# The last expert of each group is moved to the end, and its tokens are finished in slot order

## The chip, the cores and the metric

The kernel runs on one core of one Trainium2 chip. The metric is the device time of one execution in microseconds (us), the median of several runs. Before the change three runs took 882.38, 878.52 and 880.90 us: a median of 880.9.

## The reference, cut to what matters

The kernel computes one layer of a hybrid backbone (an S5 state-space branch and a convolution branch, merged, with a gated residual add), then a mixture of experts, then a final RMSNorm. The change touches only what stands behind the router. 512 tokens of 1024 channels choose one group of four and then two experts among the eight of that group:

```python
gate = jnp.sum(jax.nn.one_hot(expert_id, N_EXPERTS) * weights[..., None], axis=1)
out = jnp.zeros_like(h)
for e in range(N_EXPERTS):                      # 32 = 4 groups of 8
    act = jax.nn.silu(h @ w_gate[e]) * (h @ w_up[e])
    out = out + gate[:, e:e + 1] * (act @ w_down[e])
...
x = x + gt2 * out
return rmsnorm(x, g_final)
```

Both experts of a token lie in the same group. So a token can have at most one of the experts 7, 15, 23 and 31, the last of each group, and its other expert is then another one.

## The kernel before, in words

**Routing.** Each expert has up to 128 slots for its tokens. Tables on the chip hold, for each expert and slot, the token's row (`ix`, for gathers) and the row of its result in `ybuf` (`ixh`, for scatters; `ybuf` in device memory has two rows for each token, one for each of its experts, and is addressed in halves of 512 channels). `pw` holds the two weights of each token, `rk` its slot, `ex` its experts, `size` a size class for each expert. x after the first sub-layer lies in device memory as `x1d`, the normed and modulated rows as `h2d`.

**The expert loop** (lines 1632 to 1673, e from 0 to 32). Iteration e works on two experts at once: the down projection of expert e-1 and the gate and up projection of expert e. The orders of PE, ACT and DVE are written out by hand (`manual_schedule`, line 1621), so these three run what the loop says in the order in which it says it:

- `gather_e` (line 1397): POOL gathers the token rows of an expert two ahead into one of two buffers (`xgs`) by an indirect DMA.
- `tile_act` (1352): ACT computes Silu of the gate half, DVE multiplies by the up half, for expert e-1.
- `tile_gu` (1347): PE multiplies the tokens of expert e by its gate and up weights. An expert works in two parts of 64 slots; the second is skipped when the expert has at most 64 tokens (`halves`, 1408).
- `tile_at` (1358): PE transposes the product of `tile_act`, ACT copies it out of PSUM.
- `tile_x` (1329): PE transposes the gathered rows of expert e+1, ACT and DVE each copy one half.
- `tile_down` (1367): PE multiplies by the down weights into `pd`.
- `tile_y` and `scatter_e` (1376, 1415): DVE multiplies `pd` by the layer's output gate, POOL scatters the rows into `ybuf` by an indirect DMA. No scatter waits for another expert's scatter.

SP and POOL are not in the hand-written order. A planner puts their instructions into queues by when it expects each to be ready; a queue then runs in that order, and an instruction that waits holds up what is behind it. A size test (`halves`) on POOL is a branch: one indirect DMA for the first 64 slots, and a second one only for an expert with more.

**Weights.** `load_p(m)` issues the loads of 1 MB each on SP, three for each expert, some six experts ahead. They land in a ring of 20 places (`eraw` and `part_load`, 989 to 1022), made of several small pools of buffers; a load waits until the matmuls that read its place before are done. What the end of the kernel needs (x, the rows of `ybuf`, `g_final`) comes from the same ring. The last weight load is issued at 789.3 us.

**The end.** The results of experts 30 and 31 aren't scattered. POOL builds a one-hot matrix of slots and tokens for each (`last_prepare`, 1529), PE transposes it (`last_turn`, 1536), DVE and ACT make two parts of the weighted result (`last_y`, 1549), and PE adds these to the tokens' rows in PSUM (`fin`): x by a matmul with the identity (`last_x`, 1575), the two experts' rows by the one-hot matrix (`last_own`, 1580), the rows from `ybuf` (`last_mix`, 1587: ACT scales one row of a token, DVE adds the other, PE adds the sum). `last_rows` (1564) loads both rows of all tokens from `ybuf`, 4 loads of 1 MB on SP, after every scatter has landed. Then, for each of four blocks of 128 tokens: ACT sums squares (`last_sum`, 1594), DVE and ACT make 1/rms (`last_root`, `last_norm`), DVE scales, and SP stores 512 KB.

## Time and profile before

| | |
|---|---|
| median of 3 runs | 880.9 us |
| the profiled execution | 880.24 us |
| its span in the trace | 878.5 us |
| PE busy | 738.2 us (84%) |
| DVE busy | 458.5 us (52%) |
| ACT busy | 321.2 us (37%) |
| POOL busy | 329.6 us (38%) |
| mean granted TensorE clock | 0.959 of full speed |

The span is what the profiler recorded on the core; the device time of the same execution is 1.74 us longer. PE is TensorE, DVE VectorE, ACT ScalarE, POOL GpSimd, SP SyncE. Busy time is an average over stages with different limits, so the rows further down are taken from the stage that the change touches, the expert loop (from about 546 us) and the end.

The loop's iterations take 8.46 us each when both experts have at most 64 tokens. The down projection of expert 27 ends at 814.25 us, that of expert 31 at 849.24 us, and the span ends 29.26 us later.

### The profile page before, as it was taken

To read this page: it belongs to the slowest core of one execution; us is meant where nothing else is said; L and a number is where in the kernel's file an instruction comes from. 1 tells how busy PE (TensorE), PEld (TensorE's weight loads), DVE (VectorE), ACT (ScalarE), POOL (GpSimd) and SP (SyncE) were. 2 spreads that over 40 slices of the span, in tenths; PEclk is the share of its full clock that TensorE was granted. 3 is DMA by queue.
4 is the path that set the end of the run, shared out by engine and by line. 5 is a ranking of instruction groups with operands and counts; after the bars stand their busy time and mean duration, and the time that the engine had idled before them with its cause. 6 is when DMAs were issued, how large, how long until landed. Compare 5 with 4: busy or idle time off the path is not lost. (4 is left out here: it accounts for less than half of the span.)

```text
span 878.5 us, 14308 instructions
## 1 busy us (share of the span) xinstructions
PE 738.2 (84%) x5486; PEld 513.4 (58%) x5486; DVE 458.5 (52%) x723; ACT 321.2 (37%) x559; POOL 329.6 (38%) x293
## 2 busy tenths in 40 slices
PE   3498986998978986979999993788998998888885
PEld 0376863665656775746778872455655655555542
DVE  3948565355397798725985576133223232332344
ACT  3442621355465748526632331221112112121133
POOL 4647435345486697621610122122122122221400
PEclk9998997999989999989999996899999999999999
DMA  8916870342145454478687437999989998998042
GB/s 308 272 47 194 196 230 22 106 126 73 48 140 174 150 177 130 137 241 322 202 297 274 156 121 314 394 392 398 381 304 388 406 360 332 387 397 295 18 192 95
DMA packets 84679, 202.01 MB, mean 230 GB/s; under 512 B 12860, under 2 KB 42622, under 8 KB 74867
## 3 DMA queue, kind: packets, MB, share of 16 engines
q1 hardware_dynamic: 76754, 180.00, 57.7%
q0 software_dynamic: 5856, 12.45, 4.0%
q10 hardware_dynamic: 1984, 8.44, 3.6%
q8 instruction: 53, 0.87, 0.4%
q14 instruction: 32, 0.25, 0.1%
HBM read 180.16 MB, written 26.69 MB: 235 GB/s over the span
## 5 line engine op out<-in xcount | busy, mean ns | idle before, releaser
L1350 PE MATMUL peg<-eraw,st 128*64 128x256 f32 x1152 | 132.8, 384 | 8.4 <-PEq L1411 6.8
L1350 PEld LDWEIGHTS peg<-eraw,st 128*64 128x64 f32 x1152 | 94.1, 138 | 58.8 <-issue 33.9
L1335 DVE COPY st<-pxt 128x512 f32<-128x512 f32 x32 | 22.1, 691 | 158.7 <-PE pxt L1333 158.7
L1364 ACT ACTIVATE at<-pat 128x256 f32<-128x256 f32 x32 | 12.3, 383 | 216.0 <-PE pat L1362 216.0
L1322 POOL DMA_INDIRECT xg<-h2d,tb x32 | 30.3, 948 | 141.3 <-PE pxt L1333 129.9
L396 PE MATMUL zp<-hh,zuwh 128*128 128x512 f32 x192 | 78.2, 407 | 0.0
L398 PE MATMUL zp<-hh,zuwl 128*128 128x512 f32 x192 | 76.2, 397 | 0.5 <-POOL zuwl L757 0.4
L397 PE MATMUL zp<-hl,zuwh 128*128 128x512 f32 x192 | 76.0, 396 | 0.0
L1370 PE MATMUL ped<-eraw,at 128*64 128x512 f32 x288 | 68.9, 603 | 0.0
L98 POOL TENSOR_TENSOR adacc<-adacc,wa 128x512 f32<-128x512 f32 x30 | 47.2, 1574 | 40.9 <-ACT wa L857 38.7
L1405 POOL DMA_INDIRECT ybuf<-ye,ixh x34 | 33.9, 996 | 69.2 <-DVE ye L1380 41.6
L1380 DVE TENSOR_TENSOR ye<-ped,gt2h 128x512 f32<-128x512 f32 x60 | 39.0, 686 | 39.7 <-PE ped L1370 38.5
L1333 PE MATMUL pxt<-ident,xg 128*128 128x128 f32 x256 | 42.3, 303 | 8.5 <-DMA xg<-h2d,tb 7.7
L396 PEld LDWEIGHTS zp<-hh,zuwh 128*128 128x128 f32 x192 | 36.9, 192 | 11.7 <-issue 4.4
L398 PEld LDWEIGHTS zp<-hh,zuwl 128*128 128x128 f32 x192 | 36.7, 191 | 9.8 <-POOL zuwl L757 1.8
L1333 PEld LDWEIGHTS pxt<-ident,xg 128*128 128x128 f32 x256 | 33.6, 194 | 13.5 <-issue 9.0
L397 PEld LDWEIGHTS zp<-hl,zuwh 128*128 128x128 f32 x192 | 36.8, 192 | 7.1
L1362 PE MATMUL pat<-ident,sge 64*128 64x64 f32 x128 | 21.3, 286 | 19.0 <-PEq L1411 18.3
L1362 PEld LDWEIGHTS pat<-ident,sge 64*128 64x128 f32 x128 | 17.7, 209 | 32.8 <-PEq L1411 30.5
L1370 PEld LDWEIGHTS ped<-eraw,at 128*64 128x64 f32 x288 | 17.8, 136 | 27.2 <-issue 23.6
L98 POOL TENSOR_TENSOR vb<-vta,vtb 128x512 f32<-128x512 f32 x16 | 21.9, 1366 | 31.3 <-PE pv L533 20.2
L757 DVE TENSOR_TENSOR zuwl<-zr,zuwh 128x1024 fp32r<-128x1024 f32 x16 | 28.4, 1778 | 4.6 <-ACT zuwh L756 4.5
(499 smaller groups left out, 1652.7 us busy)
## 6 DMA issues: line engine op xcount, KB each, us to landing
eraw<-in_w_exp_gate_dram SPq DMA_DIRECT2D x24, 1024.0 KB
...
```

Source lines behind the costliest of these rows:

```text
L98: G.tensor_tensor(o, a, b, op=op)
L396: T.matmul(acc, lhsT=wh, rhs=ah, start=start, stop=False)
L397: T.matmul(acc, lhsT=wh, rhs=al, start=False, stop=False)
L398: T.matmul(acc, lhsT=wl, rhs=ah, start=False, stop=stop)
L757: (G if t in ZPOOL else V).tensor_tensor(zu[t][1], raw, zu[t][0].bitcast(F32), op=ALU.subtract)
L1322: G.indirect_dma_start(out=xg, out_offset=None, in_=h2d, in_offset=bass.IndirectOffsetOnAxis(ap=idx, axis=0), bounds_check=L - 1, oob_is_e ...
L1333: T.transpose(pt[:, k, :], xg[:, 4 * h + k:D:8], ident)
L1350: T.matmul(pg[H[c], 256 * a:256 * a + 256], lhsT=st[:, k, H[a]], rhs=r[c][k // 4][:, 256 * (k % 4):256 * (k % 4) + 256], start=(k == 0), s ...
L1362: T.transpose(pa[:, 128 * k + 64 * a:128 * k + 64 * a + 64], sg[64:128, 256 * a + k:256 * a + 256:2], ident[64:128, 64:128])
L1370: T.matmul(pd[a][H[c]], lhsT=at[:, 128 * k + 64 * a:128 * k + 64 * a + 64], rhs=r[2][k][:, 512 * c:512 * c + 512], start=(k == 0), stop=(k ...
L1380: V.tensor_tensor(y[:, 512 * a:512 * a + 512], pd[a], gt2h, op=ALU.mult)
L1405: return G.indirect_dma_start(out=ybuf.rearrange("r (c n) -> (r c) n", c=2), out_offset=bass.IndirectOffsetOnAxis(ap=ixh[:, a, e:e + 1], a ...
```

## The change: what it does

**Order.** The experts are computed in a new order (`ORD`): first the 28 that aren't the last of their group, then 7, 15, 23 and 31 (`DIR`). Weights, gathers, sizes and scatters follow this order. In the inputs these four have 9, 92, 10 and 13 tokens (counted by running the reference's router); experts 8, 9, 14 and 15 are the ones with more than 64. So expert 15 moves from place 15 to place 29.

**Results of the last four.** They aren't scattered to `ybuf`, and the one-hot matrices and the matmuls of the end (`last_prepare`, `last_turn`, `last_y`, `last_own`, `last_x`) are gone. Instead, for each of the four experts, POOL gathers in slot order: the tokens' rows of x and their weights (`own_rows`), then, once all scatters have landed, the result of each token's other expert (`own_other`). Ten indirect DMAs are issued for the first (one expert of the four needs two halves) and five for the second. Before that, four tiles of 128x2048 are cleared (`own_alloc`). DVE adds weight times other result to x (`own_base`); when the expert's down projection is done, DVE adds its weighted result and ACT sums the squares (`own_sum`); 1/rms follows (`roots`, `recip`), DVE scales and POOL scatters the rows to the output (`own_out`).

**All other tokens** are finished in token order during the last experts: `last_scale` and `last_mix` (ACT, DVE, and an add on POOL) for blocks 0 and 1 in iteration 30 and for 2 and 3 in iteration 31, `last_sum` in iterations 31 and 32, `last_out` at the end. `last_out` is now an indirect DMA on POOL whose list of rows leaves out the tokens of the last four experts.

**Tables.** `last_tables` replaces `last_weights` in iteration 1: 20 small DVE operations in place of 6, and two DMAs on SP that write the weights by result row to device memory (`pwd`).

**Places.** The loads of x and `g_final` move to the end of iteration 26, `own_alloc` and `own_rows` stand at the end of iteration 27, `last_rows` and `own_other` at the end of 28.

The diff, cut to its core (the removed functions, which stand in the code above, are left out):

```diff
+    EPG = NE // NGR
+    DIR = tuple(range(EPG - 1, NE, EPG))
+    ND = len(DIR)
+    ORD = [x_ for x_ in range(NE) if x_ not in DIR] + list(DIR)
...
-            eraws.setdefault(e, []).append(part_load((w_exp_gate, w_exp_up, w_exp_down)[m % 3][0, e], *a))
+            eraws.setdefault(e, []).append(part_load((w_exp_gate, w_exp_up, w_exp_down)[m % 3][0, ORD[e]], *a))
...
+    tok = mz2.tile([128, NT], F32, name="tok")
+    G.iota(tok, pattern=[[128, NT]], base=0, channel_multiplier=1, allow_small_or_imprecise_dtypes=True)
...
-            more[e] = nc.values_load(size[0:1, e:e + 1], engines=[EN.Pool], min_val=0, max_val=len(SIZES) - 1, skip_runtime_bounds_check_because=BYC)
-            by_size(e, lambda n: gather(xgs[e % NXG][0:n], ix[0:n, 0, e:e + 1]))
+            x_ = ORD[e]
+            more[e] = nc.values_load(size[0:1, x_:x_ + 1], engines=[EN.Pool], min_val=0, max_val=len(SIZES) - 1, skip_runtime_bounds_check_because=BYC)
+            by_size(e, lambda n: gather(xgs[e % NXG][0:n], ix[0:n, 0, x_:x_ + 1]))
...
+    ssf = mz2.tile([128, 2, 12], F32, name="ssf")
+    GRP = ((0, 6), (6, 10), (10, 12))
+    BC = (0, 1, 6, 7)
+    DC = (2, 4, 8, 10)
...
+    def after_all(ld):
+        for p_ in scattered:
+            tc.add_manual_dep(ins_of(ld), ins_of(p_).name, mybir.DependencyInfo(mybir.DependencyClass.Sync, mybir.DependencyReason.DATA), reason="results of every expert")
...
+    pwd = dram.tile([4 * L, 2], F32, name="pwd")
+    def last_tables():
+        pwt = mz2.tile([128, 2, NE], F32, tag="ixs", name="pwt", bufs=1)[:, 0].rearrange("p (q i c w) -> p q i c w", q=2, i=NT, c=2)
+        sp = mz2.tile([128, 2, NE], F32, tag="ixe", name="sp", bufs=1)
+        for q in range(2):
+            for w in range(2):
+                V.tensor_copy(pwt[:, q, :, :, w], pw[:, :, (q + w) % 2:(q + w) % 2 + 1].to_broadcast([128, NT, 2]))
+            SY.dma_start(out=bass.AP(pwd.tensor, pwd.offset + 4 * L * q, [[4, 128], [512, NT], [1, 4]]), in_=pwt[:, q].rearrange("p i c w -> p i (c w)"))
+        f = sp[:, 0, 0:24].rearrange("p (k a j) -> p k a j", k=3, a=2)
+        own["ix"] = mz2.tile([128, 3, 2, ND], I32, name="lix")
+        V.tensor_copy(f[:, 0], ixh[:, :, EPG - 1:NE:EPG])
+        V.tensor_scalar(f[:, 1], f[:, 0], float(2 * L), float(2 * L), op0=ALU.is_ge, op1=ALU.mult)
+        V.tensor_tensor(f[:, 2], f[:, 0], f[:, 1], op=ALU.subtract)
+        V.tensor_copy(own["ix"][:, 1], f[:, 2])
+        V.tensor_tensor(f[:, 2], f[:, 2], f[:, 1], op=ALU.subtract)
+        V.tensor_scalar(f[:, 2], f[:, 2], float(2 * L), None, op0=ALU.add)
+        V.tensor_copy(own["ix"][:, 2], f[:, 2])
+        V.tensor_copy(own["ix"][:, 0], f[:, 0])
+        d = sp[:, 1, 0:16].rearrange("p (k i q) -> p k i q", k=2, i=NT)
+        V.tensor_scalar(d[:, 0], ex, float(DIR[0]), None, op0=ALU.is_equal)
+        for x_ in DIR[1:]:
+            V.scalar_tensor_tensor(d[:, 0], ex, float(x_), d[:, 0], op0=ALU.is_equal, op1=ALU.add)
+        V.scalar_tensor_tensor(d[:, 1], rk, 128.0, d[:, 0], op0=ALU.is_lt, op1=ALU.mult)
+        V.tensor_tensor(d[:, 0, :, 0], d[:, 1, :, 0], d[:, 1, :, 1], op=ALU.add)
+        V.scalar_tensor_tensor(d[:, 0, :, 0], d[:, 0, :, 0], BIG, tok, op0=ALU.mult, op1=ALU.add)
+        ids["t"] = mz2.tile([128, NT], I32, name="bix")
+        V.tensor_copy(ids["t"], d[:, 0, :, 0])
     def last_loads():
         for h in range(2):
             t = eraw("x1").rearrange("p (i d) -> p i d", i=2)
             SY.dma_start(out=t, in_=x1d[256 * h:256 * h + 256].rearrange("(i p) d -> p i d", p=128))
+            x1s.extend([t[:, 0], t[:, 1]])
+        t = eraw("gfin")
+        own["gf"], own["gfh"] = t[:, 0:1024], t[:, 1024:1536]
+        SY.dma_start(out=own["gf"], in_=g_final.rearrange("(o d) -> o d", o=1).to_broadcast([128, D]))
+        for c_ in range(2):
+            SY.dma_start(out=own["gfh"][H[c_]], in_=g_final[512 * c_:512 * c_ + 512].rearrange("(o d) -> o d", o=1).to_broadcast([64, 512]))
...
+    def own_get(src, dst, k, j, rows):
+        def one(a):
+            return G.indirect_dma_start(out=dst[:, a], out_offset=None, in_=src, in_offset=bass.IndirectOffsetOnAxis(ap=own["ix"][:, k, a, j:j + 1], axis=0),
+                                        bounds_check=rows - 1, oob_is_err=False)
+        return halves(own["n"][j], one)
+    def own_alloc():
+        own["n"] = [nc.values_load(size[0:1, x_:x_ + 1], engines=[EN.Pool], min_val=0, max_val=len(SIZES) - 1, skip_runtime_bounds_check_because=BYC) for x_ in DIR]
+        own["w"] = mz2.tile([128, ND, 2, 2], F32, name="lw")
+        G.memset(own["w"], 0.0)
+        own["b"], own["y"] = [], []
+        for nm in ("b", "y"):
+            for i in range(2):
+                t = eraw("own" + nm)
+                G.memset(t, 0.0)
+                v = t.rearrange("p (j a n) -> p j a n", j=2, a=2)
+                own[nm] += [v[:, 0], v[:, 1]]
+    def own_rows(j):
+        own_get(half_rows(x1d), own["b"][j], 1, j, 2 * L)
+        own_get(pwd, own["w"][:, j], 0, j, 4 * L)
+    def own_other(j):
+        for ld in own_get(half_rows(ybuf), own["y"][j], 2, j, 4 * L):
+            after_all(ld)
+    def own_base(j):
         for a in range(2):
+            b = own["b"][j][:, a]
+            V.scalar_tensor_tensor(b, own["y"][j][:, a], own["w"][:, j, a, 1:2], b, op0=ALU.mult, op1=ALU.add)
+    def own_sum(j, pd):
+        for a in range(2):
+            b, t = own["b"][j][:, a], own["y"][j][:, a]
+            V.scalar_tensor_tensor(t, pd[a], own["w"][:, j, a, 0:1], gt2h, op0=ALU.mult, op1=ALU.mult)
+            V.tensor_tensor(b, b, t, op=ALU.add)
+        for a in range(2):
+            S.activation(own["y"][j][:, a], own["b"][j][:, a], AF.Square, accum_out=ssf[:, 0, DC[j] + a:DC[j] + a + 1])
+    def roots(g):
+        lo, hi = GRP[g]
+        d = slice(hi - (4 if g == 0 else 2), hi)
+        for c in range(2):
+            V.tensor_copy(ssf[H[c], 1, d], ssf[H[1 - c], 0, d])
+        V.tensor_tensor(ssf[:, 0, d], ssf[:, 0, d], ssf[:, 1, d], op=ALU.add)
+        S.activation(ssf[:, 1, lo:hi], ssf[:, 0, lo:hi], AF.Sqrt, bias=eps, scale=1.0 / D)
+    def recip(g):
+        lo, hi = GRP[g]
+        V.reciprocal(ssf[:, 1, lo:hi], ssf[:, 1, lo:hi])
+    stored = []
+    def no_order(ins):
+        for i_ in ins:
+            for p_ in stored:
+                tc.declare_no_dep(ins_of(i_), ins_of(p_), reason="rows of different tokens")
+        stored.extend(ins)
+    def own_out(j):
+        b = own["b"][j]
+        for a in range(2):
+            V.scalar_tensor_tensor(b[:, a], b[:, a], ssf[:, 1, DC[j] + a:DC[j] + a + 1], own["gfh"], op0=ALU.mult, op1=ALU.mult)
+        def one(a):
+            return G.indirect_dma_start(out=half_rows(out[0]), out_offset=bass.IndirectOffsetOnAxis(ap=own["ix"][:, 1, a, j:j + 1], axis=0), in_=b[:, a], in_offset=None,
+                                        bounds_check=2 * L - 1, oob_is_err=False)
+        no_order(halves(own["n"][j], one))
     def last_rows():
...
-            for p_ in scattered:
-                tc.add_manual_dep(ld.ins if hasattr(ld, "ins") else ld, (p_.ins if hasattr(p_, "ins") else p_).name, mybir.DependencyInfo(mybir.DependencyClass.Sync, mybir.DependencyReason.DATA), reason="results of every expert")
+            after_all(SY.dma_start(out=t, in_=yb))
             yrs.append(t)
...
+    def last_scale(i):
+        S.activation(yrs[i][:, 0], yrs[i][:, 0], AF.Copy, scale=pw[:, i, 0:1])
     def last_mix(i):
         y = yrs[i][:, 0]
-        S.activation(y, y, AF.Copy, scale=pw[:, i, 0:1])
         V.scalar_tensor_tensor(y, yrs[i][:, 1], pw[:, i, 1:2], y, op0=ALU.mult, op1=ALU.add)
+        gtt(x1s[i], x1s[i], y, ALU.add)
...
+        S.activation(yrs[i][:, 1], x1s[i], AF.Square, accum_out=ssf[:, 0, BC[i]:BC[i] + 1])
+    def last_out(i):
+        V.scalar_tensor_tensor(x1s[i], x1s[i], ssf[:, 1, BC[i]:BC[i] + 1], own["gf"], op0=ALU.mult, op1=ALU.mult)
+        no_order([G.indirect_dma_start(out=out[0], out_offset=bass.IndirectOffsetOnAxis(ap=ids["t"][:, i:i + 1], axis=0), in_=x1s[i], in_offset=None,
+                                       bounds_check=L - 1, oob_is_err=False)])
...
+            if e in (NE - 2, NE - 1):
+                for i in (0, 1) if e == NE - 2 else (2, 3):
+                    last_scale(i)
+                    last_mix(i)
+            if e == NE - 1:
+                for i in (0, 1):
+                    last_sum(i)
             if e == NE:
-                last_x(0)
+                recip(0)
+                for i in (0, 1):
+                    last_out(i)
+                for j in (0, 1):
+                    own_out(j)
             if e > 0:
                 at = tile_at(sg)
+            if e == NE - 1:
+                roots(0)
+                last_sum(2)
             if e == NE:
-                fin[1], fin[2] = pgs, [ps_tp(f"fin2{i}") for i in range(2)]
-                last_x(1)
-                last_x(2)
-                last["y", 0] = last_y(pd, 0)
+                last_sum(3)
+                roots(1)
             if e + 1 < NE:
                 st[e + 1] = new_st()
                 for h in range(2):
                     tile_x(xgs[(e + 1) % NXG], st[e + 1], h)
-            if e == NE - 1:
-                last_turn(0)
             if e > 0:
                 halves(wide[e - 1], lambda a: tile_down(pd, at, eraws[e - 1], a))
-            if 0 < e < NE - 1:
+            if 0 < e <= NE - ND:
                 scatter_e(e - 1, tile_y(pd))
-            if e == NE:
-                last["y", 1] = last_y(pd, 1)
-            if e == NE - 1:
-                last_turn(1)
+            if e > NE - ND:
+                if e < NE:
+                    own_base(e - 1 - NE + ND)
+                own_sum(e - 1 - NE + ND, pd)
+                if e == NE - 1:
+                    own_base(ND - 1)
             for m in range(3 * e + 19, 3 * e + 22):
                 load_p(m)
             if e == 1:
                 weights()
-                last_weights()
-            if e >= NE - 3 and e < NE - 1:
-                last_prepare(e - NE + 3)
-            if e == NE - 2:
+                last_tables()
+            if e == NE - 6:
+                last_loads()
+            if e == NE - 5:
+                own_alloc()
+                for j in range(ND):
+                    own_rows(j)
+            if e == NE - 4:
                 last_rows()
+                for j in range(ND):
+                    own_other(j)
         S.activation(rs2, rs2, AF.Sqrt)
-        fin[3] = pd
-        last_x(3)
-        for j in range(2):
-            last_own(j, last["y", j])
-        last_mix(0)
-        for i in range(NT):
-            if i + 1 < NT:
-                last_mix(i + 1)
-            last_sum(i)
-            last_root(i)
-            last_norm(i)
+        recip(1)
+        for i in (2, 3):
+            last_out(i)
+        roots(2)
+        own_out(2)
+        recip(2)
+        own_out(3)
```


## Rows read from the trace of the kernel before

**Rows 1.** The chain that ended last, in order: start us, us, what.
```profile
871.64 0.70 ACT yr L1596 x2
...
873.15 0.75 DVE x L1607
```

**Rows 2.** Windows: us, busy of PE, PEld, DVE, ACT, POOL (instructions), clock, DMA share, GB/s.
```profile
814.25:822.71 8.46, 7.45 (x53) 4.73 (x52) 2.67 (x4) 1.57 (x3) 2.78 (x3) 1.00 0.05 15
...
839.55:849.24 9.69, 9.36 (x36) 4.44 (x36) 4.90 (x7) 2.72 (x4) 0.00 (x0) 1.00 0.80 321
849.24:878.50 29.26, 16.94 (x52) 9.48 (x52) 15.65 (x25) 13.14 (x27) 0.00 (x0) 0.94 0.18 72
```

**Rows 3.** Timeline of one iteration of the expert loop: start us, us, engine line operation.
```profile
806.11 3.67 PE L1350 MATMUL peg<-eraw,st 128*64 128x256 f32 x32 [0.31 <-PEq L1411]
...
810.48 0.66 PE L1362 MATMUL pat<-ident,sge 64*128 64x64 f32 x4 [0.70 <-PEq L1411]
...
811.24 0.38 ACT L1364 ACTIVATE at<-pat 128x256 f32<-128x256 f32 x1 [6.66 <-PE pat L1362]
...
812.32 1.94 PE L1370 MATMUL ped<-eraw,at 128*64 128x512 f32 x8
...
815.62 0.69 DVE L1355 TENSOR_TENSOR sge<-peg,sge 64x512 f32<-64x512 f32 x1
```

**Rows 4.** Timeline of POOL, around two wide experts.
```profile
619.20 0.92 POOL L1322 DMA_INDIRECT xg<-h2d,tb  x1 [4.85 <-PE pxt L1333]
...
669.40 1.01 POOL L1322 DMA_INDIRECT xg<-h2d,tb  x1 [3.21 <-PE pxt L1333]
```

**Rows 5.** Timeline of POOL, near the last experts.
```profile
820.93 2.05 POOL L98 TENSOR_TENSOR xg<-oh,sel 128x512 f32<-128x512 bf16 x2 [4.66 <-PE pxt L1333]
...
824.48 1.01 POOL L1405 DMA_INDIRECT ybuf<-ye,ixh  x1 [0.15 <-issue]
```

**Rows 6.** Timeline of DVE in the loop's third iteration.
```profile
572.49 0.17 DVE L1525 TENSOR_SCALAR sel<-ex 128x8 f32<-128x8 f32 x1
...
573.69 0.69 DVE L1355 TENSOR_TENSOR sge<-peg,sge 64x512 f32<-64x512 f32 x1 [0.16 <-ACT sge L1354]
```

**Rows 7.** Groups of instructions: line engine op tiles shapes count | busy us, mean ns | idle before.
```profile
L1590 DVE SCALAR_TENSOR_TENSOR yr<-yr,pw 128x1024 f32<-128x1024 f32 x4 | 5.0, 1279 | 1.3 <-ACT yr L1589 1.3
...
L1054 DVE TENSOR_TENSOR cacc<-cacc,rs 128x512 f32<-128x512 f32 x4 | 2.5, 682 | 0.0
...
L1607 DVE SCALAR_TENSOR_TENSOR x<-fin,ssf,gfin 128x512 f32<-128x512 f32 x2 | 1.4, 748 | 0.0
```

**Rows 8.** Groups of instructions of ACT.
```profile
L1589 ACT ACTIVATE yr<-yr,pw 128x1024 f32<-128x1024 f32 x4 | 4.4, 1136 | 0.0
```

**Rows 9.** Groups of instructions of POOL.
```profile
L98 POOL TENSOR_TENSOR xg<-xg 128x512 f32<-128x512 f32 x2 | 2.5, 1272 | 0.2
...
L1255 POOL MEMSET xg<- 128x1024 f32 x2 | 1.8, 958 | 0.0
```

**Rows 10.** Timeline of ACT at the first table load in the loop.
```profile
561.75 1.28 ACT L1354 ACT_TABLE_LOAD   x1
563.04 0.59 ACT L1354 ACTIVATE sge<-peg 64x512 f32<-64x512 f32 x1
```

**Rows 11.** What is known of line 1405, the scatters: time from issue to landing.
```profile
DMA to landing us min/median/max: 2.3/7.2/9.3
```

**Rows 12.** Branches of the size tests (line 1411): ns min/median/max.
```profile
L1411 POOLq INC_SWDGE_SEM  x26: 540/1282/1740, 571.0 to 832.2; - x26
```

**Rows 13.** Windows around two idle stretches of PE; columns as in Rows 2.
```profile
552.00:554.00 2.00, 1.60 (x8) 1.57 (x8) 0.00 (x0) 0.48 (x1) 0.05 (x1) 0.50 1.00 365
...
558.00:560.00 2.00, 1.53 (x16) 0.70 (x10) 0.00 (x0) 0.00 (x0) 0.00 (x0) 1.00 1.00 408
872.00:874.00 2.00, 0.00 (x0) 0.00 (x0) 1.17 (x4) 0.62 (x3) 0.00 (x0) 1.00 0.66 262
874.00:876.00 2.00, 0.00 (x0) 0.00 (x0) 0.56 (x1) 0.00 (x0) 0.00 (x0) 0.74 0.31 125
```

77 lines of the change are left out of this document (8 added, 69 removed).

## The prediction

> **What bounds the kernel now.** I read the windows first, then the chain of waits, then timelines of single iterations. The windows of the last two iterations and of the end show PE, not DMA or DVE, as the limit of the loop: in an ordinary iteration of 8.46 us PE is busy 7.45 and DVE 2.67, at full clock and with the DMA queues almost empty (share 0.05) [rows 2]. An iteration's pace can be laid out from one timeline: the 32 gate and up matmuls take 3.67 us, the transposes of the product come 4.4 us after their start, ACT's copy and then the down projection follow, 1.94 us long [rows 3]. In what follows time is counted from the end of a down projection; the next transposes then come at 4.7 (the iteration's period taken from the down's end) and the next down at 6.5. An expert with more than 64 tokens, "wide" here, lengthens this: five iterations with two such experts took 50.20 us instead of 42.30, so 3.95 for each [rows 4].
>
> After the last down projection 29.26 us pass, and PE is busy only 16.94 of them [rows 2]. The chain there runs through the one-hot matmuls and then, block by block, through square, root, scale and store; its last links are two squares of 0.70 together with their reads, and the last scaling at 873.15 [rows 1]. This stretch is what the change replaces. The profiled execution took 880.24 us, 1.74 more than its span and 0.66 below the median of 880.9; the sum below is made against 880.24.
>
> **The end, rewritten: -13.5.** All terms are counted from the end of the down projection of the last expert but one (place 30), because DVE's hand-written list from there on is longer than PE's. An `own_sum` is two operations on PSUM of about 0.75 and two adds of 0.68 [rows 7]: 2.9. Its last square ends at 3.6. Silu now follows a Sqrt, so ACT loads a table, 1.28, then Silu 0.59 [rows 10]: 5.5. DVE's product of 0.69 [rows 3] ends at 6.2. Then come a reciprocal (0.2), two `last_out` of 1.28 and four scalings of 0.75 [rows 7]: 11.9; `roots` with three small operations of 0.2 each [rows 6]: 12.5; `own_sum` of the last expert: 15.4; two `last_out` and a reciprocal: 18.2; `roots`, `own_out`, reciprocal, `own_out` (0.6 + 1.5 + 0.2 + 1.5): 22.0. The last scatter lands 2.3 us after its issue when the queues are empty [rows 11]; the store of before ended 3.9 after its scaling (span end 878.5 against the second half of the pair that began at 873.15); I take 3.0: 25.0. PE meanwhile transposes at 6.2, ACT copies, and the last down ends at 9.2. So behind the last down stand 25.0 - 9.2 = 15.8 us instead of 29.3: -13.5. POOL's adds for x (1.27 for 512 channels [rows 9], 2.5 each) and the removed one-hot work lie beside iterations 30 and 31, where POOL has little else to do.
>
> The Trainium skill, "ScalarE: Activation LUTs", section "What ACT_TABLE_LOAD costs", puts a switch at about 2.66 us, a load of 1.28 and as much again to drain the engine. Here Silu starts at 563.04, right behind a load that began at 561.75 [rows 10], so the trace shows the load alone. By the page the one switch on the path would cost 1.4 more, and the sum would be 876.7.
>
> **The last four iterations: +3.0.** What stays of them is 8.46 for iteration 29. In 30 the squares of `own_sum` stand before Silu on ACT: 3.6 + 0.6, product at 5.0 instead of before 4.7; and two scalings of 1.14 [rows 8] stand before the copy that the down projection needs, so the down starts at 7.0 and not 6.5: 8.95. In 31 ACT's list is Silu at 4.2, two scalings (6.4), two sums of squares over 1024 channels of about 1.25 (8.9), copy 0.38 (9.3), and the down ends at 11.3. Iteration 32 ends at 9.2 as above. Sum 37.9; before, from 814.25 to 849.24, it was 35.0 [rows 2]. The removed `last_turn` and `last_x` matmuls are inside those 35.0. Expert 15's 3.95 us move from place 15 to place 29 and cancel. PE reads its weights long after they land: the DMA queues are empty from the iterations shown on [rows 2], so a wide expert that comes late takes no cover away.
>
> **The tables: +2.6.** 14 more small DVE operations, 0.2 apart as the six that they replace (572.49 to 573.69) [rows 6]: 2.8. They stand before the product that PE's transposes wait for, and that product was ready only some 0.2 before it was needed. The later iterations are PE's, so nothing gives this back. The SP queue carries two small writes behind them; weights are issued far ahead and cover that.
>
> **POOL's queue: +2 (0 to 6).** Here is the step of which the trace shows least. The first cleared tile gets its place when the down of expert place 25 ends, 16.9 us before the down of place 27 does (time zero for this paragraph). From there POOL has four clears of 1.9 (0.96 for half the size [rows 9]), ten gathers and the scatter of place 26. A scatter takes 1.0 [rows 5]; with its branch I take 1.3. Sum 21.9, so the list ends at +5. The scatter of place 27 is ready at +1. The planner orders POOL by readiness: it put the one-hot work of 820.93 before a scatter that the program has earlier, and the scatter went at 824.48 [rows 5]. All ten gathers are ready before that scatter, so I expect it behind them: at 5, landing at 7.3. Only then may `own_other` go. Queued behind on POOL is the gather of the last expert, needed at 16.9 and so covered; on SP the loads of `last_rows`. `own_base` for the first of the four stands in DVE's list before `own_sum`, which could begin at 11.2 (iteration 29 with its wide gate and up part). The gathered rows land 2.3 to 7.2 after issue [rows 11]; the 1 MB loads start at the same moment, so neither idle nor saturated: 3.5 to 4.5, and with 1.28 for `own_base` DVE is done at 12.2 to 13.2. So 1 to 2 late, 0 if the gathers are not in the way, 6 if the landing is the slow one and one more gather stands ahead. I take 2.
>
> **The clock: +1 (0 to 5).** PE now idles in iterations 30 to 32, 3 to 6 us at a time. At the end of the trace the granted clock went from 1.00 (2.4 GHz) to 0.50 (1.2 GHz) within 874 to 876, after the last matmuls near 871.6; at the loop's start it was 0.50 from 552 and 1.00 by 558 [rows 13]. [...] In 31 only a down of 1.94 follows the idle time, and in 32 DVE's list covers it. I take 1.
>
> Sum: -13.5 + 3.0 + 2.6 + 2 + 1 = -4.9, so 875.3; I say 875.
>
> **The rivals.**
> (a) Nothing is late on POOL and the clock holds: -7.9, so 872.3. For it: POOL is busy 2.78 of 8.46 us in an ordinary iteration [rows 2], and a planner that lets the scatter of place 27 through early needs only one gap. Against it: 21.9 us of work in 18.
> (b) The gain is eaten, no change: y's rows land after 7.2 and a gather stands ahead (+6), the clock falls in all three gaps (+4): +2.1 against the base of 880.24, 878 to 882. For it: the clock rows, and that DVE, PE and ACT are in fixed order, so one late landing stops all three. The rule of the Trainium skill, "TensorE: Matmul & The Clock Gate", section "Why this matters for your kernels", is to leave no PE-idle gaps between bursts, since the array falls back to its low rate; it speaks for (b).
> (c) Slower: the branches hold POOL. Behind a size test that fails stands a counting instruction of 1.28 median [rows 12]. If POOL can't issue during it, six of the eight gather pairs cost 1.28 more, the list ends at +12.7, and the gather for place 30 behind it lands near 16 while PE needs it at 8: 8 late; then the scatter, `own_other` and its landing come about 5 later than `own_base` can bear, and the clock falls (4). -7.9 + 17: 889. It decides once lateness and clock together exceed 7.9. Against it: scatters and gathers of before show no such spacing on POOL's own timeline, where the work of 820.93 to 824.48 is dense [rows 5].
> (d) The change doesn't shorten the end, because the stores of the six indirect DMAs on POOL follow one another late: each takes 1.0, and DVE produces one every 0.7 to 1.3, so it could cost 2 at most; it is inside the range.
>
> **Chances.** Forecast (871.5 to 878.5) 0.46, (a) and below 0.22, (b) 0.20, (c) 0.12. Its own range is 871.5 to 878.5; with (a) whole and most of (b) the range is 869.5 to 882.5. A measurement of this kernel can tell about 0.5%, 4.4 us, from no change: the forecast lies below 876.5 three times in four. Faster 0.35 + 0.22, same 0.11 + 0.20, slower 0.12.
>
> **What would show it.** In the changed kernel's trace: between the last down and the span's end 15.8 us, DVE without pause but for Silu's table load; iteration 31 of about 11.3, ended by ACT's copy; the product of iteration 2 late by 2.6; the scatter of place 27 behind the gathers of `own_rows`, 5 us after its down; `own_base` of the first expert waiting on a DMA for 1 to 2 us. Wrong would be: PE waiting for gathered tokens at place 30 or 31 (then c), `own_base` waiting over 5 us (b), or an end over 18 us (a term of DVE mis-sized).

## The result, and the profile after

The changed kernel takes 907.9 us (median of 4 runs, 907.7 to 910.5) against 880.4 for the kernel before on the same chip (878.5 to 882.4): 1.032 times as long, 95% interval 1.029 to 1.035. The prediction said 875. The profiled execution spans 905.5 us, 27.0 more than that of before.

Three starts of PE's matmuls divide a span: the first gate and up product (place 0), the down product of place 27, that of place 31. In the changed kernel's timeline of PE they are these (start us, us, engine, line, operation):

```profile
553.13 4.88 PE L1358 MATMUL peg<-eraw,st 128*64 128x256 f32 x32
...
817.99 1.94 PE L1378 MATMUL ped<-eraw,at 128*64 128x512 f32 x8
...
878.61 3.68 PE L1378 MATMUL ped<-eraw,at 128*64 128x512 f32 x8 [0.53 <-ACT at L1372]
```

All profiled executions are laid out by these starts (differences in us; A ahead of the loop, B places 0 to 27, C to place 31, D from its down product to the end). Every A here belongs to nearly the same program and still differs by 6 us, so causes are read from B, C and D. Runs 8, 10, 14 and 16 are laid out in the same way where they are told.

| profiled execution | A | B | C | D | span |
|---|---|---|---|---|---|
| before | 554.3 | 258.1 | 35.0 | 31.2 | 878.5 |
| order alone (run 5) | 556.5 | 254.3 | 38.9 | 31.3 | 881.0 |
| **changed** | 553.1 | 264.9 | 60.6 | 26.9 | 905.5 |
| 1 weights late | 552.2 | 257.7 | 73.3 | 27.2 | 910.4 |
| 2 first pair early | 551.2 | 264.6 | 56.5 | 27.3 | 899.6 |
| 3 adds on DVE | 555.7 | 261.0 | 58.2 | 26.7 | 901.6 |
| 6 weights in the middle, pair early | 555.0 | 258.2 | 56.2 | 27.3 | 896.6 |
| 7 and gathers unconditional | 555.3 | 257.0 | 50.5 | 28.7 | 891.5 |
| 9 and adds on DVE | 557.1 | 257.5 | 47.9 | 28.6 | 891.1 |
| 12 and list spread | 553.7 | 254.7 | 46.5 | 28.8 | 883.6 |
| 15 and POOL's last stores taken off | 552.7 | 256.6 | 46.6 | 19.4 | 875.3 |

Run 5 has the new order of experts with the old end, so it is the base: the change costs 10.6 us in B and 21.7 in C, and gains 4.4 in D. The prediction counted from the end of the last down product: there the end takes 23.2 us (882.3 to 905.5) in place of 29.3, a gain of 6.1 where 13.5 were forecast.

**B.** The timeline of POOL, early in the loop (in brackets the idle time ahead and what ended it):

```profile
569.52 1.03 POOL L1414 DMA_INDIRECT ybuf<-ye,ixh  x1 [1.77 <-DVE ye L1388]
585.03 1.07 POOL L1578 DMA_INDIRECT lw<-pwd,lix  x1 [14.48 <-DMA pwd<-pwt]
...
590.72 0.91 POOL L1330 DMA_INDIRECT xg<-h2d,tb  x1 [0.30 <-issue]
...
594.56 1.02 POOL L1414 DMA_INDIRECT ybuf<-ye,ixh  x1 [0.30 <-issue]
```

The program asks for the token weights (`lw`) in iteration 27. Their index list is there from iteration 2 on, so the planner put the gathers there. They wait 14.48 us for the landing of SP's small write of the weight table, which was issued at 571.30, while the DMA engines are busy throughout with the experts' weights (mean share 1.06 from 574.3 to 584.5). On POOL's in-order queue the token gather of 590.72 and the scatter of 594.56 wait with them. PE shows both losses of B, the table's DVE work at 575 and the late tokens at 597:

```profile
575.14 0.66 PE L1370 MATMUL pat<-ident,sge 64*128 64x64 f32 x4 [2.72 <-DVE sge L1363]
...
597.37 0.71 PE L1370 MATMUL pat<-ident,sge 64*128 64x64 f32 x4 [4.44 <-remote]
```

The profile names the second releaser only as `remote`. That it is the tokens shows in run 2, which has the same gathers there and names them:

```profile
595.65 1.94 PE L1341 MATMUL pxt<-ident,xg 128*128 128x128 f32 x8 [4.27 <-DMA xg<-h2d,tb]
```

**C.** POOL again, after place 27, and what DVE and PE then wait for:

```profile
821.29 1.01 POOL L1414 DMA_INDIRECT ybuf<-ye,ixh  x1 [0.30 <-DVE ye L1388]
826.08 1.05 POOL L1578 DMA_INDIRECT owny<-ybuf,lix  x1 [3.77 <-issue]
831.04 1.01 POOL L1578 DMA_INDIRECT owny<-ybuf,lix  x1 [3.92 <-DMA ownb<-x1d,lix]
...
835.99 1.82 POOL L1590 MEMSET ownb<- 128x2048 f32 x1
...
840.72 1.01 POOL L1578 DMA_INDIRECT ownb<-x1d,lix  x1 [0.30 <-issue]
```
```profile
842.31 1.41 DVE L1607 SCALAR_TENSOR_TENSOR ownb<-owny,lw,ownb 128x512 f32<-128x512 f32 x2 [12.36 <-DMA ownb<-x1d,lix]
...
848.73 0.71 PE L1370 MATMUL pat<-ident,sge 64*128 64x64 f32 x4 [13.66 <-DVE sge L1363]
...
850.44 6.09 POOL L98 TENSOR_TENSOR eraw<-eraw,yr 128x1024 f32<-128x1024 f32 x2 [8.71 <-DVE yr L1662]
...
852.18 4.89 DVE L1607 SCALAR_TENSOR_TENSOR ownb<-owny,lw,ownb 128x512 f32<-128x512 f32 x2
...
863.78 5.63 POOL L98 TENSOR_TENSOR x<-x,yr 128x1024 f32<-128x1024 f32 x2 [7.26 <-DVE yr L1662]
...
864.93 4.51 DVE L1622 COPY ssf<-ssf 64x4 f32<-64x4 f32 x2
```

The tile of the first pair (experts 7 and 15) is cleared at 835.99, behind all gathers of `ybuf`, and its x1 rows come last. `own_base(0)` waits 12.36 us for them, and the product that PE needs stands behind it in DVE's list, so PE waits 13.66. Two later DVE pairs last 4.89 and 4.51 us instead of 1.41 and 0.34; POOL is adding 128x1024 blocks then.

**D.** Windows of iteration 31 (its first row) and of what follows, columns as in [rows 2], whose last row is the end of before:

```profile
855.40:869.50 14.10, 8.03 (x46) 3.43 (x42) 12.09 (x11) 6.57 (x12) 6.75 (x3) 0.76 0.01 1
869.50:882.30 12.80, 4.39 (x13) 1.32 (x12) 11.23 (x17) 7.36 (x13) 2.81 (x2) 0.63 0.07 26
882.30:896.30 14.00, 0.00 (x0) 0.00 (x0) 9.52 (x19) 3.30 (x8) 7.75 (x7) 0.50 0.33 126
896.30:905.50 9.20, 0.00 (x0) 0.00 (x0) 0.00 (x0) 0.00 (x0) 0.00 (x0) 0.50 0.00 0
```

In the last 9.2 us no engine computes and no transfer runs. The rows of the program's last line tell what does: there the queue of each engine closes with DRAIN instructions (queue, operation, count, ns min/median/max, first and last start). First the changed kernel, then the kernel before:

```profile
L1787 POOLq DRAIN  x3: 46/99/8317, 896.3 to 905.2; - x3
```
```profile
L1713 POOLq DRAIN  x3: 46/103/6606, 833.9 to 878.3; - x3
```

POOL's closing drain lasted 6.6 us in the kernel before. It ran from 833.9 to 840.5, right behind POOL's last scatter, with 38 us of the program still to come. Now POOL's last scatter is issued at 893.4, behind DVE's last scaling, and 8.3 us of drain follow it:

```profile
890.79 1.42 DVE L1642 SCALAR_TENSOR_TENSOR ownb<-ownb,ssf,gfin 128x512 f32<-128x512 f32 x2
...
893.36 0.97 POOL L1645 DMA_INDIRECT out_dram<-ownb,lix  x1 [0.30 <-issue]
```

### The profile page after: what moved, and what is told of

It reads as the page before. It is cut to its first block, busy times and chain, and to the rows that moved or that the text cites. A ratio compares the mean times of both kernels' runs of the same rounds, so it can differ in the third digit from the quotient of the medians.

```text
span 905.5 us, 14271 instructions
## 1 busy us (share of the span) xinstructions
PE 723.1 (80%) x5398; PEld 502.6 (56%) x5398; DVE 477.7 (53%) x753; ACT 324.5 (36%) x564; POOL 366.2 (40%) x318
## 5 line engine op out<-in xcount | busy, mean ns | idle before, releaser
L1378 PE MATMUL ped<-eraw,at 128*64 128x512 f32 x288 | 75.0, 650 | 3.6 <-ACT at L1372 3.6
L1370 PE MATMUL pat<-ident,sge 64*128 64x64 f32 x128 | 21.3, 289 | 49.0 <-DVE sge L1363 27.2
L1388 DVE TENSOR_TENSOR ye<-ped,gt2h 128x512 f32<-128x512 f32 x56 | 36.4, 687 | 38.5 <-PE ped L1378 37.2
L1414 POOL DMA_INDIRECT ybuf<-ye,ixh x31 | 30.9, 998 | 57.8 <-DVE ye L1388 37.1
L1341 PE MATMUL pxt<-ident,xg 128*128 128x128 f32 x256 | 44.6, 314 | 9.5 <-DMA xg<-h2d,tb 7.8
L1378 PEld LDWEIGHTS ped<-eraw,at 128*64 128x64 f32 x288 | 19.1, 147 | 34.0 <-issue 26.9
```

The source lines that it names most:

```text
L1341: T.transpose(pt[:, k, :], xg[:, 4 * h + k:D:8], ident)
L1370: T.transpose(pa[:, 128 * k + 64 * a:128 * k + 64 * a + 64], sg[64:128, 256 * a + k:256 * a + 256:2], ident[64:128, 64:128])
L1378: T.matmul(pd[a][H[c]], lhsT=at[:, 128 * k + 64 * a:128 * k + 64 * a + 64], rhs=r[2][k][:, 512 * c:512 * c + 512], start=(k == 0), stop=(k ...
L1388: V.tensor_tensor(y[:, 512 * a:512 * a + 512], pd[a], gt2h, op=ALU.mult)
L1414: return G.indirect_dma_start(out=ybuf.rearrange("r (c n) -> (r c) n", c=2), out_offset=bass.IndirectOffsetOnAxis(ap=ixh[:, a, ORD[e]:ORD[ ...
```

## The experiments

Runs 1 to 3, 6 to 10, 12 and 14 to 16 change the changed kernel, runs 4, 5, 11 and 13 the kernel before. Ratios are to the kernel before, run on the same chip, with 95% intervals.

**Run 1, weights late.**
```
-        G.memset(own["w"], 0.0)
+        G.tensor_scalar(own["w"].rearrange("p j a w -> p (j a w)"), xgs[1][:, 0:4 * ND], 0.0, 0.0, op0=ALU.mult, op1=ALU.add)
```


> The changed kernel, with one edit: the small table of token weights (lw) is no longer cleared by a memset but by a multiplication that reads the gathered tokens of place 29, so its gathers can't be put into POOL's queue before that gather. Theory (POOL's in-order queue): the wait of 14.48 us at 585 us in front of the first weight gather is gone, the tokens of places 4 to 6 come in time, the end of the down product of place 27 moves from 819.9 to about 809 us, and the run goes from 907.9 to about 897 us. Rival 1 (the loss before place 27 comes from the new order of the experts and its weights' DMA, or from the twenty DVE operations of the tables): the wait on POOL goes but the down product of place 27 stays at 817 us or later, and the run stays at 904 to 909. Rival 2 (the loss is given back later, since the last four iterations wait for gathers that start by the ring's release): place 27 comes at 809 but the run stays above 902.

912.8 us, 1.038 (1.036 to 1.041): as rival 2 has it. The wait of 14.48 us is gone and B falls by 7.1, as the theory says; but the gathers now stand in front of the last clears and gathers, each branch past a second half holds POOL (3.29 and 4.38 us below; its two counting instructions, `INC_SWDGE_SEM`, take 1.6 to 1.7 each), and C grows by 12.7. POOL, and what DVE waits for:

```profile
804.85 1.09 POOL L1578 DMA_INDIRECT lw<-pwd,lix  x1 [3.29 <-DMA eraw<-x1d]
810.32 1.04 POOL L1578 DMA_INDIRECT lw<-pwd,lix  x1 [4.38 <-DMA xg<-h2d,tb]
```
```profile
846.88 1.41 DVE L1607 SCALAR_TENSOR_TENSOR ownb<-owny,lw,ownb 128x512 f32<-128x512 f32 x2 [25.02 <-DMA ownb<-x1d,lix]
```

So POOL's queue decides in both places.

**Run 2, first pair early.**
```
             if e == NE - 6:
+                own_alloc()
                 last_loads()
             if e == NE - 5:
-                own_alloc()
```


> The changed kernel with one edit: the four tiles of the own rows are taken from the ring one iteration earlier, ahead of the tiles for x1 and the final gain. In the order of POOL's queue the clear of the first pair's tile and its four gathers of x1 rows then stand three places earlier, ahead of the gathers of ybuf. Theory: own_base(0) no longer waits 12.36 us for x1 rows at 842 us, and the product of the next iteration no longer waits 13.66 us; place 27's down to place 31's down falls from 62.4 to about 50 us and the run from 907.9 to about 895 us. Rival (own_base(0) then waits as long for the gathers of ybuf, or DVE slowed beside POOL's additions takes the gain): 902 to 908, with a wait of DVE on own rows of over 6 us still there.

901.8 us, 1.025 (1.022 to 1.028). C falls by 4.1 only. The wait for x1 rows is gone and the rival's is there, on the gathers of `ybuf`:

```profile
836.00 1.42 DVE L1607 SCALAR_TENSOR_TENSOR eraw<-owny,lw,eraw 128x512 f32<-128x512 f32 x2 [8.26 <-DMA owny<-ybuf,lix]
```

**Run 3, adds on DVE.**
```
-        gtt(x1s[i], x1s[i], y, ALU.add)
+        V.tensor_tensor(x1s[i], x1s[i], y, op=ALU.add)
```


> The changed kernel with one edit: the four additions of x1 to the weighted results of the plain tokens (128 x 1024 each) run on DVE instead of POOL. Theory (DVE and POOL hinder each other): in the changed kernel a pair of own_base operations took 4.89 us instead of 1.41 and a pair of copies of 64 x 4 took 4.51 us instead of 0.34 while POOL added, 7.7 us in all on the path; these go, four additions of about 1.3 us come onto DVE, of which half stand in the way of the next product: 907.9 falls to 902 to 905, and no small DVE operation of the last three iterations lasts over 1 us. Rival (the slow DVE rows are waits on something else, or lie beside the waits for gathers): the slow rows stay, and the run is 908 to 913.

902.4 us, 1.025 (1.021 to 1.029). The slow rows are gone:

```profile
853.36 1.41 DVE L1607 SCALAR_TENSOR_TENSOR ownb<-owny,lw,ownb 128x512 f32<-128x512 f32 x2
...
865.12 0.34 DVE L1622 COPY ssf<-ssf 64x4 f32<-64x4 f32 x2
```

C falls by 2.4; 7.7 us of slowing less 4.9 for the four adds would give 2.8. Another 3.9 us of the profiled gain are in B, where the edit changes nothing: by luck the weight table landed earlier, and POOL waited 13.37 us for it and not 14.48. In run 9 the same edit brings 2.5 in C.

**Run 5, the order alone.** The same edit stands in the gathers, the scatters, the size tests and the one-hot's expert numbers of the kernel before.
```
-            eraws.setdefault(e, []).append(part_load((w_exp_gate, w_exp_up, w_exp_down)[m % 3][0, e], *a))
+            eraws.setdefault(e, []).append(part_load((w_exp_gate, w_exp_up, w_exp_down)[m % 3][0, ORD[e]], *a))
```


> The kernel before, with only the new order of the experts (experts 7, 15, 23 and 31 at places 28 to 31, their weights loaded in that order); the end and its tables are as before. Theory: the order costs nothing by itself, since expert 15's second product only moves from place 15 to place 29: 879 to 882 us, and the first scatters follow each other as in the kernel before. Rival (the new order of the weights' DMA or of the large experts costs part of the 27 us): 885 us or more.

882.5 us, 1.001 (0.998 to 1.003). Expert 15's second half moves 3.8 us from B to C, and the sum of B, C and D stays within 0.3 us.

**Runs 6 and 7, weights in the middle and pair early; own gathers unconditional.**
```
+            if e == 12:
+                own_weights(xgs[(e + NXG) % NXG])     # clear and gathers of lw
```
```
-        return halves(own["n"][j], one)               # in own_get, run 7
+        return [one(0), one(1)]
```
Run 6:

> The changed kernel with the first pair's tile taken early, as in the run before it, and the gathers of the token weights tied to the gather of place 14, so that they stand in the middle of POOL's queue, where neither the weight table is awaited nor the last four places are near. Theory: the two delays add up; down of place 27 comes 7 us earlier than in the changed kernel (as with the weights late), and the last four iterations stay as with the pair early: 901.8 - 7 = 893 to 896 us. Rival (what POOL gains early is lost again at a later bound, such as the landing of gathers behind the weights): 899 to 903.

Run 7:

> As the run before it (weights in the middle, pair early), and the gathers of the own rows, weights and other results always run both halves instead of branching past the second half of an expert with 64 tokens or fewer. A half skipped costs two semaphore increments of 1.7 to 1.9 us on POOL (3.9 to 4.1 us between the first and the second gather of ybuf), a half without valid rows one issue of about 1.3 us. Theory (these increments hold POOL's queue): own_base(0) starts 2 to 3 us earlier and the run is 2 to 3 us shorter than without this edit. Rival (the landing of the last gather is set by the 4 MB of yr loads that SP issues at the same time, 10 us at some 420 GB/s): no change within 1 us.

Run 6: 895.2 us, 1.016 (1.012 to 1.019). With run 2's C and run 1's B, the two delays add up. Run 7: 892.5, 1.012 (1.008 to 1.016). The median falls by 2.7 us, as expected. In the profiled executions C falls by 5.7, twice that, and D grows by 1.4; POOL's closing drain there lasts 9.1 us in place of 8.3. In run 2 two increments held POOL between the first and the second gather of `ybuf`; without them DVE waits 1.66 where it had waited 8.26 (7.90 in run 6). The row of the increments in run 2, then DVE's in run 7:

```profile
L1420 POOLq INC_SWDGE_SEM  x2: 1895/1898/1900, 823.9 to 826.0; - x2
```
```profile
825.98 0.79 DVE L1611 SCALAR_TENSOR_TENSOR eraw<-owny,lw,eraw 128x512 f32<-128x512 f32 x1 [1.66 <-DMA owny<-ybuf,lix]
```

**Runs 8 and 9, loads behind the gathers.** Run 9 is run 7 with run 3's edit; run 8 also puts the `yr` loads behind the gathers of `ybuf` (collected in `own["got"]`) and makes them wait for these.
```
             after_all(ld)
+            for p_ in own["got"]:
+                tc.add_manual_dep(ins_of(ld), ins_of(p_).name, mybir.DependencyInfo(mybir.DependencyClass.Sync, mybir.DependencyReason.DATA), reason="behind the rows of the last experts")
```
Run 8:

> As the run before it, with two more edits: the four loads of yr (4 MB) wait for the own gathers of ybuf, and the additions to x1 run on DVE (alone, on the changed kernel, they brought about 5.5 us). Theory (the gathers landed behind the loads): the gathers of ybuf land within 3 us of their issue, own_base(0) starts about 4 us earlier, and with 5 us for the additions the run comes to 9 us below the one before it, near 883 us. Rival (the yr loads then come late: the scaling of the first plain block waits for them in iteration 30): at most 5 us below, with ACT waiting for yr by over 2 us.

Run 9:

> The changed kernel with weights in the middle, pair early, own gathers unconditional, and the additions to x1 on DVE, with the yr loads back at their old place. Theory (DVE is slowed beside POOL's additions, 7.7 us, less what its own additions cost): 5 us below the run without the additions on DVE (892.5), 886 to 889. Rival (the gain of the additions on DVE seen in the changed kernel lay beside a wait that is gone now): 891 to 893.

892.8 and 892.3 us, 1.015 (1.011 to 1.019) and 1.012 (1.008 to 1.017): neither below run 7. In run 8 the theory's part came (`own_base(0)` waits no more) and the rival's took it back, ACT waiting for `yr`; C is 52.4, above run 7's:

```profile
833.20 1.15 ACT L1666 ACTIVATE yr<-yr,pw 128x1024 f32<-128x1024 f32 x1 [6.25 <-DMA yr<-ybuf]
```

Run 9's C is 2.5 below run 7's; its times, with a later loop start, don't resolve that.

**Runs 4, 11 and 13, the drain in the kernel before.** The last of the four stores on POOL (run 4); no store, but a copy at the very end (run 11); that copy and 16 small stores on POOL in iterations 8 to 23 (run 13).
```
-        SY.dma_start(out=out[0, 128 * i:128 * i + 128], in_=xi)
+        (G if i == NT - 1 else SY).dma_start(out=out[0, 128 * i:128 * i + 128], in_=xi)
```
```
+        if i == NT - 1:
+            gcopy(yrs[i][:, 0, 0:64], xi[:, 960:1024])
```
```
+                if 7 < e < 24:
+                    G.dma_start(out=dump[128 * (e - 8):128 * (e - 8) + 128], in_=y_[:, 0:64])
```
Run 4:

> The kernel before with one edit: the store of the last of the four blocks of the output is issued on POOL's queue instead of SP's. Theory (a drain of POOL at the end of the program starts only when its last transfer is done): POOL's drain of 6.6 us, which ran unseen from 834 us in the kernel before, now follows the last store; the run goes from 880.4 to 886 to 890 us. Rival (the 8.3 us of drain at the end of the changed kernel belong to its scatters or to the profile alone): 880 to 882.5, with the drain short or hidden.

Run 11:

> The kernel before with a copy of 128 x 64 on POOL that reads the last scaled block, at the very end. It is no transfer. Theory (the drain follows POOL's last instruction of any kind): the drain of 6 to 7 us moves behind this copy and the run goes up by 4 us, as with the last store on POOL (884 to 886). Rival (the drain belongs to POOL's transfers, and is over long before): POOL's drain at the end is under 1 us and the run stays within 1.5 us of 879.5.

Run 13:

> The kernel before with the copy on POOL at the very end, as in the run with a POOL operation at the end, and with 16 small stores on POOL's queue (128 rows of 64 floats each, into a scratch tensor), one in each of iterations 8 to 23, where POOL idles 4 us and more per iteration. They add some 16 x 144 = 2300 packets to the 5856 of the software queue. Theory (the drain's length goes with the packets that POOL's queues had in the whole program: 6.6 us at 5856, 7.3 at 6000, 8.3 at 7552, 9.05 at 8128): the drain at the end grows from 6.9 to about 9.3 us, and the run by as much, to 886 to 888. Rival (its length goes with what is in flight at the end, or with the gathers by index): the drain stays at 6.6 to 7.3 us and the run at 884.

884.7 us, 1.007 (1.005 to 1.010); 884.5, 1.005 (1.002 to 1.007); 887.2, 1.008 (1.006 to 1.011). The drain of each, in this order:

```profile
L1713 POOLq DRAIN  x3: 46/115/7341, 874.2 to 882.1; - x3
```
```profile
L1715 POOLq DRAIN  x3: 46/109/6912, 878.2 to 885.7; - x3
```
```profile
L1719 POOLq DRAIN  x3: 46/109/8222, 876.9 to 885.7; - x3
```

A copy of 0.24 us at the end brings the drain onto the path as a store does: it follows POOL's last instruction of any kind. And since the time of the whole execution grows, the drain is no artifact of the profile. Run 13 is a half miss. The drain grew by 1.3 us, not 2.4, and the stores added 512 packets, not 2300. Packets alone don't set its length: run 5 has the 5856 packets of the kernel before, and its drain takes 7.7 us and not 6.6.

**Runs 10 and 12, the end without POOL, and the list spread.** Run 10's edit stands in `last_out` for blocks 2 and 3 as well; of run 12's the loop's part is shown. Run 12 also moves the gathers of the token weights behind place 16 and lets the stores of own rows run both halves.
```
-        no_order(halves(own["n"][j], one))
+        if j < 2:
+            no_order(halves(own["n"][j], one))
+        else:
+            for a in range(2):
+                SY.dma_start(out=dump[128 * j + 64 * a:128 * j + 64 * a + 64].rearrange("r (c n) -> (r c) n", c=2), in_=b[:, a])
```
```
                 sg = tile_act(pgs[(e - 1) % 2])
+            if e == NE - 2:
+                own_base(0)
+            if e > NE - ND + 1:
+                own_sq(e - 2 - NE + ND)
...
                 own_sum(e - 1 - NE + ND, pd)
+                if e == NE - 2:
+                    own_base(1)
+                if e == NE - 1:
+                    own_base(ND - 2)
+                    own_base(ND - 1)
...
+            if e == 12:
+                last_tables()
```
Run 10:

> As the run before it, but the last stores (the plain blocks 2 and 3 and the own rows of experts 23 and 31) go by SP as plain stores into a scratch tensor; their rows of the output are not written. POOL's last transfer is then that of expert 15. Theory (POOL's drain of 8.3 us starts when its last transfer is issued and is done, so it now runs beside the last chain): the drain ends within 2 us of the last store's landing, and the run is 5 to 7 us shorter than the run before it, near 881. Rival (the landing of the last stores ends the run whichever queue has them): at most 2 us shorter.

Run 12:

> As the run with three repairs, and the manual order mended: the tables are built in iteration 12, while the product of 109 tokens covers DVE, instead of iteration 1; the base of expert 7 is added one iteration later, that of the others right behind the sum before it, where DVE waited 1.39 us for the activation; the squares of the own rows stand behind the next activation; the stores of own rows run both halves. Theory (what is left of the loss is DVE's and POOL's order, and the drain): 3.5 us for the tables, 3 to 4 us for the base of expert 7, 2 to 3 us for the 1.4 us waits, so 877 to 880, about the kernel before, with the drain still on the path. Rival (the clock, or the landing of yr, takes it): 883 or more.

Run 10: 879.5 us, 0.998 (0.996 to 1.001), 1.4% below run 9, without two blocks and two experts' rows of the output; D falls by 9.3, more than the 5 to 7 expected. From DVE's last scaling to the span's end 15.1 us pass in run 9 and 5.8 in run 10; the 15.1 hold 2.1 in which POOL issues its last transfers, 3.1 until the drain starts, 9.1 of drain and 0.8 behind it. Run 12 puts the tables into iteration 12, `own_base(0)` into iteration 30, the other bases behind the sum before them and the squares behind Silu: 884.0 us, 1.005 (1.002 to 1.007), as its rival has it. B is 254.7, near that of run 5 and 2.8 below run 9's: the tables had cost about 3. C fell by 1.5 and not by 5 or more. Two rows of PE's last downs and one of DVE show part of what holds C now:

```profile
830.47 5.35 PE L1378 MATMUL ped<-eraw,at 128*64 128x512 f32 x16
...
843.90 3.26 PE L1378 MATMUL ped<-eraw,at 128*64 128x512 f32 x8 [3.66 <-ACT at L1372]
...
847.20 0.75 DVE L1617 SCALAR_TENSOR_TENSOR ye<-ped,lw,gt2h 128x512 f32<-128x512 f32 x1 [1.16 <-PE ped L1378]
```

The down of place 30 waits for ACT, then runs partly at half clock (0.57 granted in the mean), and DVE waits 1.16 us for it. Place 29's lasts 5.35 us against 3.65 in run 5.

**Runs 14 to 16.** Run 14 is run 12 with run 10's edit; runs 15 and 16 are runs 14 and 12 with the weights' gathers at place 22.
```
-            if e == 14:
+            if e == 20:
                 own_weights(xgs[(e + NXG) % NXG])
```
Run 14:

> As the run with the list spread, but the last stores (plain blocks 2 and 3, own rows of experts 23 and 31) go by SP as plain stores into a scratch tensor; their rows of the output are not written. Theory (what is left of the loss is POOL's end: 7 transfers in a row from 863.5 us, 1.3 us each, and the drain of 8 to 10 us behind the last of them): 10 to 12 us below the run with the list spread, 872 to 875, faster than the kernel before by about 5 us, which is what the prediction worked out for the change without these costs. Rival (PE's half clock and DVE's list set the end of the last iterations): 878 or more.

Run 15:

> As the run with the list spread and the last stores on SP (plain blocks 2 and 3 and the own rows of experts 23 and 31 into a scratch tensor, their rows of the output not written), with the gathers of the token weights behind the gather of place 22 instead of 16. That run lost 10.9 us in the middle of the loop, at two places where PE's own queue stood 6.0 and 3.7 us. Theory (these stalls come from what POOL gathers at that moment, eight small gathers around the tokens of a place): the stretch to the down product of place 27 takes 255 us again and the run comes to 873 to 877. Rival (the stalls belong to PE's program or to the order of SP's loads, and stay): 884 to 887.

Run 16:

> As the run with the list spread, which writes all of the output, with the gathers of the token weights behind the gather of place 22 instead of 16. Theory: nothing else changes, so 883 to 885 us, 0.3 to 0.6% above the kernel before, the same 9 us of POOL's drain behind the last scatter; if the eight gathers cost the loop something at place 16, up to 2 us less. Rival (the place of these gathers decides over stalls of PE): a stretch to the down product of place 27 that differs from 254.7 us by over 3 us.

Run 14: 886.6 us, 1.008 (1.005 to 1.010), a miss. C and D are as the theory says (46.4 and 19.3), but B is 265.6. PE's own queue stood still at the branch of the products twice, 5.95 and 3.67 us, the first time so:

```profile
725.06 0.71 PE L1370 MATMUL pat<-ident,sge 64*128 64x64 f32 x4 [5.95 <-PEq L1420]
```

Run 15: 877.4, 0.996 (0.994 to 0.997), 0.4% below the kernel before, with part of the output in the scratch tensor. Both stalls are gone, as its theory has it, but run 12 has its gathers where run 14 has them and no such stall. POOL's drain still ends the run: SP's queue closes at 872.0, POOL's drain lasts from 864.3 to 874.4, and no engine computes and no transfer runs in the last 3.3 us of the span (875.3):

```profile
L1812 POOLq DRAIN  x3: 46/105/10098, 864.3 to 875.0; - x3
L1812 SPq DRAIN  x3: 7/7/13, 872.0 to 874.7; - x3
```

Run 16, which writes the whole output: 891.0, 1.011 (1.010 to 1.013), slower than run 12, as its rival has it. B is 3.7 longer in the profiled execution; eight small gathers stood in front of a place's token gather, and PE waited for it. By their ratios runs 12 and 16 differ by 0.6%, some 6 us; what the rest of it is no profile shows.

```profile
757.49 1.94 PE L1341 MATMUL pxt<-ident,xg 128*128 128x128 f32 x8 [2.96 <-DMA xg<-h2d,tb]
```

In run 15 PE waited 1.3 us there. No version that writes the whole output beat the kernel before; run 12 comes nearest. What held PE's queue in run 14 stays open.

## Why the prediction was wrong

The sum went wrong at three of its terms: the last landing (3.0 us, 13.3 came), POOL's queue (+2, some 17 came) and the last four iterations (+3.0, over 7 came without any of POOL's delays). C's 21.7 us come apart as 4.1 for the pair taken late (run 2), 5.7 for the increments (run 7), 2.5 for DVE beside POOL's adds (run 9), 1.5 for the order of DVE's list (run 12), 7.6 that no run removed, and 0.3 between runs 2 and 6. Even the dearest rival on record, 889, lay below the 907.9 that came.

- **The end, -13.5: the list was right, what follows it was not.** From the end of place 30's down (869.50) to DVE's last scaling (892.2) the changed kernel takes 22.7 us; 22.0 were worked out. Silu starts at 875.90, right behind a table load of 1.28 that began at 874.61, as in [rows 10]:

```profile
874.61 1.28 ACT L1362 ACT_TABLE_LOAD   x1
875.90 0.59 ACT L1362 ACTIVATE sge<-peg 64x512 f32<-64x512 f32 x1
```

But 3.0 were allowed for the last landing, and 13.3 came: 2.1 to the end of the last scatter's issue, 2.0 until the drain starts, 8.3 of drain, 0.9 to the span's end. The last down also ended at 12.8 of this count and not at 9.2. The end of over 18 us that was named as a sign stood for a mis-sized term of DVE; it was POOL's. The drain stands in no chain of waits of the kernel before, only in the rows of the last line's queue. Run 10 confirms the term: without POOL's last transfers D falls by 9.3.

- **POOL's queue, +2: the largest miss.** The prediction knew that the planner orders POOL by readiness [rows 5], and used it for one scatter. Applied to the gathers of `lw` it would have sent them to iteration 2, where they cost B 7.1 (run 1); and it would have asked when the first pair's tile comes free, which the planner put last of all. In C this queue cost about 10 us: 4.1 for the pair (run 2), 5.7 for the increments (run 7). `own_base` waited 12.36, the sign that was named for rival (b).
- **Rival (c) had part of the mechanism.** POOL does hold during the increments behind a size test that fails. They were priced at 1.28 each from [rows 12]; at the end of the loop a skipped half costs two of 1.9. But they made `own_base` late, not the tokens of places 30 and 31, for which PE did not wait in the changed kernel. The rival got 0.12, since in the kernel before nothing that was due stood behind such a test.
- **The tables, +2.6.** About 3 came: 3.4 by run 1 against run 5, 2.8 by run 12 against run 9. PE waited 2.72 us for the product where it waits 0.71 in the kernel before (the row below) and in run 5, so the product came 2.0 late; the 20 operations took 3.3 us, less than 0.2 each. The rest is PE's clock, which was at 0.65 in the mean over the next down: it lasted 2.94 instead of 1.94.

```profile
574.64 0.66 PE L1362 MATMUL pat<-ident,sge 64*128 64x64 f32 x4 [0.71 <-DVE sge L1355]
```

- **The last four iterations, +3.0.** ACT's list was priced and DVE's was not. With all of POOL's delays removed C is still 7.6 above run 5 (run 12). There iteration 31 takes 11.3 us from down to down, as priced, and its down waits for ACT's copy; but iteration 30 takes 4.2 more than in run 5, where 0.5 were forecast, and iteration 32 takes 11.2, not 9.2. In the changed kernel's iteration 31 DVE is busy 12.09 of 14.10 us: two mixes (2.5), the rest of a base pair that POOL's adds had slowed (1.7), a sum (2.9), a product (0.7) and the copies, which lasted 4.5 beside POOL's adds. Those adds were costed at nothing, beside iterations 30 and 31; by run 3 they cost 2.4 net of what they take on DVE. How much of the 7.6 is DVE's list, ACT's or PE's clock no run tells.
- **The clock, +1.** No row shows this term. At the loop's start [rows 13] PE ran from 552.4 to 557.5 at 0.50, so that burst lost some 2.5 us, an estimate. In the changed kernel both last downs ran at 0.50 (1.2 GHz): 3.68 us each against 1.94. But the downs had ended, at 869.50 and 882.30, when DVE, busy without pause, came to the sums that read them, at 870.99 and 883.27. So these 3.5 us are not on the path there:

```profile
865.82 3.68 PE L1378 MATMUL ped<-eraw,at 128*64 128x512 f32 x8 [3.08 <-ACT at L1372]
...
870.99 0.75 DVE L1612 SCALAR_TENSOR_TENSOR owny<-ped,lw,gt2h 128x512 f32<-128x512 f32 x1
...
883.27 0.75 DVE L1612 SCALAR_TENSOR_TENSOR owny<-ped,lw,gt2h 128x512 f32<-128x512 f32 x1
```

With DVE's list spread they begin to be: DVE's wait of 1.16 us in run 12.

- **Where it was right, and where by luck.** Run 15 against run 5: B +2.3, C +7.7, D -11.9, together -1.9 where -4.9 was forecast for everything. The rewritten end is worth something once POOL's last work ends earlier. That run 15's median lies 4.2 us below the kernel before, close to the forecast, is in part luck: its terms are others, and part of its output goes to a scratch tensor.
